# Moving the matrix combinations, a third gate and the squares of a group norm around the end of a state-space mixer

## The chip, the cores and the metric

The kernel runs on one core of a Trainium2 chip. A core has a matrix engine (TensorE, PE in the profile; PEld is its weight load), a vector engine (VectorE, DVE), an activation engine (ScalarE, ACT), GpSimd (POOL) and a sync engine (SP) that mostly issues transfers; a transfer can be issued from the SP, ACT and POOL queues. Each engine runs its own queue in the order in which the program was built, and waits on semaphores of the others. The metric is the device time of one execution in microseconds (us), as the median of several executions.

## The reference: what is computed

One layer of an encoder trunk on 512 prompt tokens and 64 sample tokens (T = 576 columns), with d_model 1024, everything in fp32. One wide projection of the normed input feeds three branches, which are merged and projected:

```python
proj = rmsnorm(x) @ w_in        # 1024 x 13344, split into
# glu_v, glu_g, conv_gate, z, xbc, dt_raw, q, xa_gate, gates
u = glu_v * sigmoid(glu_g)                       # branch A
c = causal_dwconv31(u)
c = silu(layernorm(c)) * silu(conv_gate); out_a = c @ conv_out_w
y = ssd_scan(silu(conv4(xbc)), dt, ...)          # branch B, 4 groups of 512 channels
y = (y + xh * D) * silu(z)
yg = y * rsqrt(mean(y * y, per group of 512))    # grouped RMS norm
out_b = (yg * ssd_norm_w) @ ssd_out_w
out_c = (attention(q, mem) * silu(xa_gate)) @ xa_out_w   # branch C
m = g0 * out_a + g1 * out_b + g2 * out_c
out = x + rmsnorm(m @ w_out)
```

## The kernel before

**Tiles.** Channels lie on the 128 partitions, tokens along the free dimension, so a projection onto 128 output channels is one "job": a weight tile of 1024 x 128 against the normed input `hT` (8 blocks of 128 rows by 576 tokens). Every fp32 operand is split into a high and a low part (`hi`/`lo`, `whi`/`wlo`, `hT[0]`/`hT[1]`), and `mac` (L214) issues three products for each block, on two halves of 288 tokens: 48 matmuls of 128 x 288 for a job. `W(name)` (L207) hands out a job's weights and prepares those of the job two places further in the list `order`: a load on SP into `raw`, a copy to `whi` on ACT (L193), and then `wlo`, either by a subtraction on DVE (L195) or by a copy on ACT (L197) and an accumulating transfer that POOL issues (L198). Each of these tiles has three buffers.

**Stages.** First the four groups g = 0 to 3 of the state-space mixer, each of five chunks (`chunk_a`, `chunk_b`; the last matmuls of a chunk are those of L603, into `pd`). Between the chunks stand `fills`: jobs for the gate z, the next group's B, C and x, and, for g = 3, the output projections of group 2 (`out_b(2, q)`, jobs `ob2_0` to `ob2_3`) and three gated units of branch A (`glu(j)`: jobs `gg{j}` and `gv{j}`, a tanh on ACT, a product on DVE into the tile `u`). A finished `u` puts the 31 taps of its depthwise convolution into the list `bg`; `bgrun(n)` takes the next n of them and gives them a low priority, so that they fill DVE's time (L760, here called taps). 240 taps are to be done before branch A's layer norm.

Behind the last chunk of a group stand `gating_a(g)` (y times z on DVE, L635; squares on ACT, summed on DVE into `tot`, L641; `tot` split into `th` and `tl`) and `gating_b(g)`: the sum over channels by matmuls with ones (L666, L667), a square root on ACT (L669), a reciprocal on DVE (L674), four scalings on DVE (L678) and the splits into `hi` (ACT, L620) and `lo` (DVE, L622). `out_b(3, q)`, jobs `ob3_0` to `ob3_3`, multiply these. For g = 3 the jobs `cg0` to `cg2` of the convolution's gate (`cg_spill`, with L827 on ACT and L828 on DVE) stand around `gating_b(3)`, and `cg3` behind `ob3_3`.

**Combinations.** Thirty-four jobs that follow (`gg3` to `gv7`, the gates g1 and g2, the attention's gate) are computed in pairs with seven half-sized products instead of eight (`product`, L950). This needs four sums and differences of quarters of `hT`, `T1` to `T4`: DVE adds (L852), subtracts (L861 to L869), and each result is split (`put`: ACT L857, DVE L858). The loop over `kp` does this in two halves, before `out_b(3, 0)`.

**Behind it** come the pairs, the attention over four heads, the projections `oc0` to `oc7` with `merge`, then `cg7` and `g0_0` to `g0_7`, under which the layer norm of branch A runs: the sum `csum` goes through ones matmuls (`ln_sum`, L1322 and L1323) to a mean (L1328), squares, a second `ln_sum`, a square root (L1340), a reciprocal (L1341), and eight products that are split for `oa0` to `oa7`. The last stage is `w_out` and the closing norm.

**Order.** The program text gives priorities; a list scheduler places each instruction on its engine, except where the text pins it (`keep_in_program_order`, as for the taps). So an edit of the text can also move instructions that it does not name.

Of the kernel before, what the change touches and what calls it, by code (L numbers as in the profile page):

```python
# [8 lines left out]
F32 = mybir.dt.float32  # L9
# [6 lines left out]
T = 576  # L16
# [12 lines left out]
def hybrid_trunk_kernel(  # L29
# [9 lines left out]
    nc = tc.nc  # L39
# [51 lines left out]
    spill = {k: dram.tile([8, 128, T], F32, name=f"spill_{k}") for k in ("xg", "g2", "cg")}  # L91
# [25 lines left out]
    def glu_jobs(j):  # L117
        wjob(f"gg{j}", w_in, C_GG + 128 * j)
        wjob(f"gv{j}", w_in, C_GV + 128 * j)

    for g in range(4):
        f = [("z", 4 * g + j) for j in range(4)]
        if g > 0:
            f += [("o", q) for q in range(4)]
        if g < 3:
            f += [("B", g + 1), ("C", g + 1), ("x", 4 * g + 4), ("x", 4 * g + 5)]
        f.sort(key=lambda e: "zBoCx".index(e[0]))
        if g == 3:
            z_, o_ = f[:4], f[4:]
            f = [("u", 0), z_[0], ("u", 1), z_[1], o_[0], z_[2], ("u", 2), o_[1], z_[3], o_[2], o_[3]]  # L130
        fills.append(f)
        for k, i in f:
            if k == "z":
                z_job(i)
            elif k == "o":
                ob_job(g - 1, i)
            elif k == "u":
                glu_jobs(i)
            else:
                wjob(f"{k}{i}", w_in, {"B": C_B, "C": C_C, "x": C_X}[k] + 128 * i)  # L140
        if g < 3:
            for j in (4 * g + 6, 4 * g + 7):
                wjob(f"x{j}", w_in, C_X + 128 * j)

    for j in range(3):
        wjob(f"cg{j}", w_in, C_CG + 128 * j)
    for q in range(4):
# [90 lines left out]
    def v2(ap):  # L238
# [4 lines left out]
    s2 = st.enter_context(tc.tile_pool(name="s2", bufs=2, reuse_waits="tile"))  # L243
# [11 lines left out]
        out=mask, in_=mask, pattern=[[1, 128]], compare_op=ALU.is_ge, fill=0.0,  # L255
# [75 lines left out]
    def tr_act(tiles, k, dst, wcol, ncols):  # L331
# [18 lines left out]
        out=after, in_=after, pattern=[[-1, 128]], compare_op=ALU.is_ge, fill=0.0,  # L350
# [280 lines left out]
    def gating_a(g):  # L631
        ys = [gx[4 * g + j][:, 0:T] for j in range(4)]
        tot = s2.tile([128, T], F32, tag="tot", name="tot", bufs=1)
        for j in range(4):
            nc.vector.tensor_tensor(ys[j], ys[j], gz[4 * g + j], ALU.mult)  # L635
            if j == 0:
                nc.scalar.activation(tot, ys[j], AF.Square)
            else:
                sq = s2.tile([128, T], F32, tag="gsq", name="gsq", bufs=1)
                nc.scalar.activation(sq, ys[j], AF.Square)  # L640
                nc.vector.tensor_tensor(tot, tot, sq, ALU.add)  # L641
        th = hl[0].tile([128, T], F32R, tag="hi", name="th")
        tl = hl[0].tile([128, T], F32R, tag="lo", name="tl")
        nc.scalar.activation(th, tot, AF.Copy)
        nc.vector.tensor_tensor(tl, tot, th.bitcast(F32), ALU.subtract)
        gtot[g] = (ys, th, tl)
# [61 lines left out]
    def bgrun(n):  # L708
        with tc.high_priority(offset=-150):
            for _ in range(min(n, len(bg))):  # L710
                bg.pop(0)()
# [21 lines left out]
    def glu(j, pool, tag, bufs):  # L733
        pg = proj(f"gg{j}", HB)
        t = pool.tile([128, T], F32, tag=tag, name=tag, bufs=bufs)
        nc.scalar.activation(v2(t[:, 0:512]), pg[:, :, 0:256], AF.Tanh, scale=0.5)
        nc.scalar.activation(t[:, 512:T], pg[:, 1, 256:320], AF.Tanh, scale=0.5)
        pv = proj(f"gv{j}", HB)

        def gate(a, b):  # L740
            nc.vector.scalar_tensor_tensor(v2(a), v2(t[:, 0:512]), 1.0, pv[:, :, 0:256], ALU.add, ALU.mult)
            nc.vector.scalar_tensor_tensor(b, t[:, 512:T], 1.0, pv[:, 1, 256:320], ALU.add, ALU.mult)

        u_tile(j, t, gate)
# [31 lines left out]
    def push_conv(*js):  # L776
        for ops in zip(*[conv_ops(j) for j in js]):
            bg.extend(ops)
# [10 lines left out]
    for g in range(4):  # L789
        f = [lambda k=k, i=i: fill_job(g, k, i) for k, i in fills[g]]  # L790
# [33 lines left out]
    def cg_spill(j):  # L824
        pt = proj(f"cg{j}")
        t = sx.tile([128, 640], F32, tag="bc", name="bc", bufs=4)[:, 0:T]
        nc.scalar.activation(v2(t), va(pt), AF.Tanh, scale=0.5)  # L827
        nc.vector.scalar_tensor_tensor(v2(t), v2(t), 1.0, va(pt), ALU.add, ALU.mult)  # L828
        nc.scalar.dma_start(out=spill["cg"][j], in_=t)
        bgrun(3)  # L830

    cg_spill(0)
    gating_b(3)
    cg_spill(1)
# [5 lines left out]
        return hT[0][:, ks, ts], hT[1][:, ks, ts]  # L840

    comb = {k: tuple(tcp.tile([128, 4, 288], F32R, name=f"{k}{a}", bufs=1) for a in "hl") for k in ("T1", "T2", "T3", "T4")}
    for kp in range(2):
        ks = slice(2 * kp, 2 * kp + 2)

        def blk(i, j):
            if j == 1:
                f = s2.tile([128, 582], F32, tag="xp", name="xp")[:, 0:T].rearrange("p (k t) -> p k t", k=2)
            else:
                f = s2.tile([128, T], F32, tag="acc", name="f", bufs=2).rearrange("p (k t) -> p k t", k=2)  # L850
            h, l = hb(i, j)
            nc.vector.tensor_tensor(f, h[:, ks].bitcast(F32), l[:, ks].bitcast(F32), ALU.add)  # L852
            return f

        def put(name, f):
            h, l = comb[name]
            nc.scalar.activation(h[:, ks], f, AF.Copy)  # L857
            nc.vector.tensor_tensor(l[:, ks], f, h[:, ks].bitcast(F32), ALU.subtract)  # L858

        a, b = blk(0, 1), blk(0, 0)  # L860
        nc.vector.tensor_tensor(b, b, a, ALU.subtract)  # L861
        put("T1", b)
        c = blk(1, 1)
        nc.vector.tensor_tensor(a, c, a, ALU.subtract)
        put("T3", a)
        nc.vector.scalar_tensor_tensor(c, b, -1.0, c, ALU.mult, ALU.subtract)
        put("T2", c)
        d = blk(1, 0)
        nc.vector.scalar_tensor_tensor(d, c, -1.0, d, ALU.mult, ALU.subtract)  # L869
        put("T4", d)  # L870
    for q in range(4):
        out_b(3, q)
        bgrun(2)
    st.close()
    cg_spill(3)

# [153 lines left out]
    for p in range(np_):  # L1032
        f = at[p, "P2"]
# [51 lines left out]
    for s, dst in ((0, o_csp), (1, o_css)):  # L1085
# [4 lines left out]
        for r in range(3):  # L1090
            nc.sync.dma_start(
                out=dst[0, 0, r].rearrange("(j c) -> j c", c=128), in_=tb[24 * r:24 * r + 24]
# [100 lines left out]
    def att_scores(h, khi, klo, qhi, qlo, ckh, ckl):  # L1193
        vv = token_major(None, o_mv, h, v_proj(h))
        vhl = hilo(a1, [128, 2, 256], "vv", vv)
        Ps = []
        for tp in range(3):
            ps = ps_tile()
            cnt = 2 if tp < 2 else 1
            n = 128 if tp < 2 else 64  # L1200
            for t in range(cnt):
                t0 = 256 * tp + 128 * t
                kh_, kl_ = (khi, klo) if tp < 2 else (ckh, ckl)
                mac1(
                    ps[:n, 256 * t:256 * t + 256],
                    [(qhi[:, i, t0:t0 + n], qlo[:, i, t0:t0 + n], kh_[:, i], kl_[:, i]) for i in range(2)],
                )
            Ps.append(softmax(ps, n, cnt))
            bgrun(2)
        return vhl, Ps  # L1210

    def att_pt(h, Ps):
# [89 lines left out]
    def merge(j, br, gname, oname, act, ob=ob):  # L1302
        if gname is None:
            t = sx.tile([128, 640], F32, tag="bc", name="bc", bufs=4)[:, 0:T]
            nc.sync.dma_start(out=t, in_=spill["g2"][j])
        else:
            t = gname
        pt = proj(oname, act=act)
        bgrun(5)
        nc.vector.scalar_tensor_tensor(v2(t), v2(t), 1.0, va(pt), ALU.add, ALU.mult)  # L1310
        nc.vector.tensor_tensor(ob[:, j], ob[:, j], t, ALU.add)

# [13 lines left out]
    def ln_mean():  # L1326
        for pt, (s, n) in zip(ln_sum(), HA):
            nc.scalar.activation(mean[:, s:s + n], pt[:, :n], AF.Copy, scale=1.0 / D)  # L1328
        for j in range(8):
            nc.vector.tensor_tensor(cact[j], cact[j], mean, ALU.subtract)  # L1330
            if j == 0:
                nc.scalar.activation(csum, cact[j], AF.Square)
            else:
                sq = e2.tile([128, NC], F32, tag="lsq", name="lsq")[:, 0:T]
                nc.scalar.activation(sq, cact[j], AF.Square)
                nc.vector.tensor_tensor(csum, csum, sq, ALU.add)
# [8 lines left out]
    sgs = {4 + i: t for i, t in enumerate(sgl)}  # L1345
# [5 lines left out]
        else:  # L1351
            g0t.append(gate_t(f"g0_{j}", 0, j, hlA, "lo", 8))

    for j in range(4):
        sgs[j] = hlA.tile([128, T], F32, tag="hi", name="hi", bufs=8)
        nc.sync.dma_start(out=sgs[j], in_=spill["cg"][j])
    bgrun(10000)
    late_job(*late[0])
    late_job(*late[1])
    ln_mean()  # L1360
    for e in late[2:5]:
        late_job(*e)
    ln_rstd()
# [155 lines left out]
```

## Time and profile before

| | |
|---|---|
| median of 3 runs | 1129.82 us (1129.18 to 1131.78) |
| the profiled execution, its own time | 1130.53 us |
| its span, first to last instruction | 1128.8 us |
| PE busy | 1091.0 us (97%) |
| DVE busy | 862.8 us (76%) |
| ACT busy | 607.7 us (54%) |
| POOL busy | 133.2 us (12%) |
| mean granted TensorE clock | 0.989 of full speed |

Busy time is the sum over instructions of an engine, with overlaps counted once; the rest of the span is idle. The granted clock has two levels, 1.00 (2.4 GHz) and 0.5 (1.2 GHz). A row of a timeline gives the start and the length in us, the engine, the line, the operation, output<-inputs, shapes and how many; in brackets, where there was one, the idle time ahead of it and what ended it.

### The profile page before, as it was taken

The page shows a single profiled execution, that of the slowest core. Times are in us where ns is not written, and L with a number is a line of the kernel's source. Part 1 is how long each engine was busy: PE and PEld are TensorE (multiplying, and loading weights), DVE is VectorE, ACT ScalarE, POOL GpSimd, SP SyncE. Part 2 cuts the span into 40 slices and gives each one's busy share as a digit, 9 for nine tenths or more (in the row PEclk, how much of TensorE's full clock was granted, in tenths as well). Part 3 has the DMA queues.
Part 4 walks back from the last instruction along what each step waited for, and adds up shares of the span by engine and source line. Part 5 has one row for each costly group of instructions (what it writes and reads, how often), then busy time and mean ns, then how long its engine had stood idle before and what let it go on. Part 6 is the DMA issues. An engine that isn't in the chain of part 4 may idle for free.

```text
span 1128.8 us, 20472 instructions
## 1 busy us (share of the span) xinstructions
PE 1091.0 (97%) x8081; PEld 1047.3 (93%) x8081; DVE 862.8 (76%) x1370; ACT 607.7 (54%) x1069; POOL 133.2 (12%) x230
## 2 busy tenths in 40 slices
PE   8999999999999999968998999999999999999997
PEld 8999999999999999968998999999899999999974
DVE  5778898578867878796888989849788789475533
ACT  5654675456437642362666576656445733674331
POOL 0100120012002100012121331100000111111000
PEclk9999999999999999988999999999999999999999
DMA  7354433442354633473867767757556889868912
GB/s 206 95 156 124 138 114 104 127 117 80 95 144 112 149 96 99 113 172 74 191 177 203 161 145 199 208 164 198 151 155 159 185 225 223 201 161 184 252 39 84
DMA packets 202213, 168.74 MB, mean 149 GB/s; under 512 B 15014, under 2 KB 175822, under 8 KB 202118
## 3 DMA queue, kind: packets, MB, share of 16 engines
q1 hardware_dynamic: 188294, 128.77, 39.4%
q0 software_dynamic: 12096, 35.13, 17.2%
q10 hardware_dynamic: 1728, 3.54, 0.8%
q8 instruction: 63, 1.03, 0.4%
q14 instruction: 32, 0.26, 0.1%
HBM read 117.08 MB, written 15.21 MB: 117 GB/s over the span
## 4 chain that ended last, share of the span: by engine, by line
PE 85%; DVE 6%; DMA 4%; ACT 2%; issue 1%; SPq 0%; DVEq 0%; ACTq 0%; POOLq 0%
PE mm L218 51%; PE X L950 9%; PE Y L950 5%; PE ps L218 4%; PE ps L1165 2%; PE ps L1166 2%; PE Z L950 2%; PE ps L1164 2%; PE ps L577 2%; PE ps L603 1%; PE ps L581 1%; DVE c L760 1%; DMA ob<-in_x_prompt_dram 1%; PE ps L542 1%; DMA wlo<-raw 1%
## 5 line engine op out<-in xcount | busy, mean ns | idle before, releaser
L218 PE MATMUL mm<-hT,whi 128*128 128x288 f32 (+2 forms) x2240 | 399.4, 298 | 1.7 <-ACT ob L689 0.7
L218 PEld LDWEIGHTS mm<-hT,whi 128*128 128x128 f32 x2240 | 334.2, 189 | 5.6 <-issue 2.2
L218 PE MATMUL mm<-hT,wlo 128*128 128x288 f32 (+2 forms) x1120 | 246.2, 298 | 0.0
L193 ACT ACTIVATE whi<-raw 128x1024 fp32r<-128x1024 f32 x118 | 124.7, 1057 | 196.5 <-PE mm L218 166.1
L760 DVE SCALAR_TENSOR_TENSOR c<-u,dww,c 128x606 f32<-128x606 f32 x240 | 202.1, 845 | 2.3
L218 PEld LDWEIGHTS mm<-hT,wlo 128*128 128x128 f32 x1120 | 184.7, 189 | 0.8 <-issue 0.6
L218 PE MATMUL mm<-hi,whi 128*128 128x288 f32 x512 | 112.2, 301 | 8.1 <-ACT hi L620 7.8
L195 DVE TENSOR_TENSOR wlo<-raw,whi 128x1024 fp32r<-128x1024 f32 x68 | 83.0, 1220 | 41.4 <-ACT whi L193 41.4
L218 PE MATMUL mm<-lo,whi 128*128 128x288 f32 x512 | 110.8, 298 | 1.6 <-DVE lo L622 1.6
L218 PE MATMUL mm<-hi,wlo 128*128 128x288 f32 x512 | 110.6, 297 | 0.8 <-DMA wlo<-raw 0.8
L218 PEld LDWEIGHTS mm<-hi,whi 128*128 128x128 f32 x512 | 83.1, 191 | 9.4 <-ACT hi L620 8.1
L198 POOL DMA_DIRECT2D wlo<-raw x50 | 43.9, 878 | 389.5 <-ACT wlo L197 286.7
L218 PEld LDWEIGHTS mm<-lo,whi 128*128 128x128 f32 x512 | 83.4, 190 | 1.9 <-DVE lo L622 1.9
L218 PEld LDWEIGHTS mm<-hi,wlo 128*128 128x128 f32 x512 | 83.2, 189 | 1.2 <-DMA wlo<-raw 1.0
L197 ACT ACTIVATE wlo<-raw 128x1024 fp32r<-128x1024 f32 x50 | 52.4, 1048 | 21.9 <-PE ps L218 21.9
L470 DVE SCALAR_TENSOR_TENSOR acc<-xp,scw,acc 128x579 f32<-128x579 f32 x72 | 58.3, 814 | 5.2 <-ACT acc L466 4.1
L917 ACT ACTIVATE ph<-rawb 128x512 fp32r<-128x512 f32 x34 | 21.5, 632 | 52.1 <-PE Z L950 22.4
L933 DVE TENSOR_TENSOR wlo<-sm,whi 128x1024 fp32r<-128x1024 f32 x34 | 41.5, 1220 | 4.5 <-ACT whi L932 4.4
L462 POOL COPY tails<-xp 128x3 f32<-128x3 f32 x24 | 18.3, 762 | 191.7 <-ACT xp L460 186.4
L932 ACT ACTIVATE whi<-sm 128x1024 fp32r<-128x1024 f32 x34 | 35.9, 1056 | 7.3 <-PE X L950 3.5
L691 DVE TENSOR_TENSOR ob<-ob,mm 128x576 f32<-128x576 f32 x24 | 18.0, 751 | 19.7 <-PE mm L218 19.6
L563 ACT ACTIVATE M<-R,tok 128x128 f32<-128x128 f32 (+1 forms) x80 | 24.8, 380 | 13.1 <-PE ps L603 13.1
(375 smaller groups left out, 2248.6 us busy)
## 6 DMA issues: line engine op xcount, KB each, us to landing
raw<-in_w_in_dram SPq DMA_DIRECT2D x70, 512.0 KB
wlo<-raw POOLq DMA_DIRECT2D x50, 512.0 KB, 5.6
raw<-in_w_in_dram SPq DMA_DIRECT2D x34, 256.0 KB
rawb<-in_w_in_dram SPq DMA_DIRECT2D x34, 256.0 KB
R<-scr SPq DMA_DIRECT2D x16, 512.0 KB
raw<-in_ssd_out_w_dram SPq DMA_DIRECT2D x16, 512.0 KB
raw<-in_xa_kv_w_dram SPq DMA_DIRECT2D x16, 512.0 KB
pl<-raw POOLq DMA_DIRECT2D x17, 256.0 KB, 3.7
```

The source lines that it names most:

```text
L193: a = nc.scalar.activation(hi[:, :n_], raw[:, :n_], AF.Copy)
L195: b = nc.vector.tensor_tensor(lo[:, :n_], raw[:, :n_], hi[:, :n_].bitcast(F32), ALU.subtract)
L197: nc.scalar.activation(lo[:, :n_], raw[:, :n_], AF.Copy, scale=-1.0)
L198: nc.gpsimd.dma_start(out=lo[:, :n_], in_=raw[:, :n_], accum_op=ALU.add)
L218: m = nc.tensor.matmul(o, lhsT=w, rhs=r[:, s:s + w_], start=(i == 0 and a == 0), stop=(i == n - 1 and a == 2),)
L470: nc.vector.scalar_tensor_tensor(acc, xp[:, r:r + 579], w4[:, r, jt:jt + 1], acc, ALU.mult, ALU.add)
L563: nc.scalar.activation(M[:, 4 + e, :], R[:nl, 4 + e, :], AF.Relu, scale=-1.0, bias=tok[:nl, 0, c, a + 4:a + 5])
L577: nc.tensor.matmul(pS, lhsT=bt[:nl], rhs=xw[:nl], start=True, stop=True)
L760: nc.vector.scalar_tensor_tensor(c, upad[j][:, r:r + NC], w31[:, r, j:j + 1], c, ALU.mult, ALU.add)
L932: nc.scalar.activation(hi, sm, AF.Copy)
L933: nc.vector.tensor_tensor(lo, sm, hi.bitcast(F32), ALU.subtract)
L950: nc.tensor.matmul(o, lhsT=w[:, k], rhs=r[:, k], start=(start and k == 0 and a == 0), stop=(k == 3 and a == 2), skip_group_check=True,)
```

## The change

Five edits:

- The gated unit `glu(2)` (96 matmuls) leaves the fills of g = 3 and stands behind the last chunk and `gating_a(3)`, ahead of `cg_spill(0)`; its weights move in `order` accordingly.
- The squares of the group norm for j = 2 go into a tile of their own (`gsq2`, in the buffers of `acc`), so that they alternate with `gsq`.
- The two halves of the combinations become a function `combine(kp)`, called behind `out_b(3, 0)` and `out_b(3, 1)` in the text.
- Taps: none inside `cg_spill` and `out_b(3, q)`, three behind `cg_spill(3)`; in the attention's scores 3, 3 and 2 instead of 2, 2 and 2; six instead of five in each merge.
- The four loads of `cg` tiles from DRAM stand behind `ln_mean()` instead of ahead of the rest of the taps.

```diff
-            f = [("u", 0), z_[0], ("u", 1), z_[1], o_[0], z_[2], ("u", 2), o_[1], z_[3], o_[2], o_[3]]
+            f = [("u", 0), z_[0], z_[1], ("u", 1), o_[0], z_[2], o_[1], z_[3], o_[2], o_[3]]
...
+    glu_jobs(2)
     for j in range(3):
         wjob(f"cg{j}", w_in, C_CG + 128 * j)
...
-                sq = s2.tile([128, T], F32, tag="gsq", name="gsq", bufs=1)
+                if j == 2:
+                    sq = s2.tile([128, T], F32, tag="acc", name="gsq2", bufs=2)
+                else:
+                    sq = s2.tile([128, T], F32, tag="gsq", name="gsq", bufs=1)
...
         nc.scalar.dma_start(out=spill["cg"][j], in_=t)
-        bgrun(3)
-
+
+    glu(2, s2, "acc", 2)
+    push_conv(2)
     cg_spill(0)
     gating_b(3)
...
-    for kp in range(2):
+    def combine(kp):
         ks = slice(2 * kp, 2 * kp + 2)
...
     for q in range(4):
         out_b(3, q)
-        bgrun(2)
+        if q < 2:
+            combine(q)
     st.close()
     cg_spill(3)
+    bgrun(3)
...
             Ps.append(softmax(ps, n, cnt))
-            bgrun(2)
+            bgrun(3 if tp < 2 else 2)
...
         pt = proj(oname, act=act)
-        bgrun(5)
+        bgrun(6)
...
-    for j in range(4):
-        sgs[j] = hlA.tile([128, T], F32, tag="hi", name="hi", bufs=8)
-        nc.sync.dma_start(out=sgs[j], in_=spill["cg"][j])
     bgrun(10000)
     late_job(*late[0])
     late_job(*late[1])
     ln_mean()
+    for j in range(4):
+        sgs[j] = hlA.tile([128, T], F32, tag="hi", name="hi", bufs=8)
+        nc.sync.dma_start(out=sgs[j], in_=spill["cg"][j])
```

What the scheduler makes of it, at three places (lines of the changed kernel are 1 to 8 higher).

PE, from the last matmul ahead of the norm's sums in group 3 to the first output projection, before; `hT` matmuls are those of `cg2`, `hi` and `lo` those of `ob3_0`:

```order
L218 MATMUL mm<-hT_93,whi 128x288 x2
L218 MATMUL mm<-hT_92,wlo 128x288 x2
L666 MATMUL ps<-th,onesr 128x288 x2
L667 MATMUL ps<-tl,onesr 128x288 x2
L218 MATMUL mm<-hi,whi 128x288 x4
L218 MATMUL mm<-lo,whi 128x288 x2
```

The same sums in the changed kernel, where the first three rows end `cg0` and the `hT` rows behind L670 begin `cg1`:

```order
L219 MATMUL mm<-hT_92,whi 128x288 x2
L219 MATMUL mm<-hT_93,whi 128x288 x2
L219 MATMUL mm<-hT_92,wlo 128x288 x2
L670 MATMUL ps<-th,onesr 128x288 x2
L219 MATMUL mm<-hT_92,whi 128x288 x2
L219 MATMUL mm<-hT_93,whi 128x288 x2
L219 MATMUL mm<-hT_92,wlo 128x288 x2
L219 MATMUL mm<-hT_92,whi 128x288 x2
L219 MATMUL mm<-hT_93,whi 128x288 x2
L219 MATMUL mm<-hT_92,wlo 128x288 x2
L219 MATMUL mm<-hT_92,whi 128x288
L671 MATMUL ps<-tl,onesr 128x288 x2
```

Behind the last chunk PE now has, in this order: 11 matmuls left of `gg2` and 48 of `gv2`, `cg0`, the sums of `th`, 13 of `cg1`, the sums of `tl`, the other 35 of `cg1`, `cg2`, `ob3_0`. Ahead of the last chunk's L603 it has 37 matmuls of `gg2` where it had all 96 of `gg2` and `gv2`.

DVE, up to the low parts for `ob3_0` in the kernel before; `rs` is the group norm's factor, `xs` the gated outputs, `c` a tap:

```order
L828 SCALAR_TENSOR_TENSOR bc<-bc,mm 128x576
L869 SCALAR_TENSOR_TENSOR f<-xp,f 128x576
L645 TENSOR_TENSOR tl<-tot,th 128x576
L760 SCALAR_TENSOR_TENSOR c<-u,dww,c 128x606
L858 TENSOR_TENSOR T2l<-xp,T2h 128x576
L858 TENSOR_TENSOR T4l<-f,T4h 128x576
L760 SCALAR_TENSOR_TENSOR c<-u,dww,c 128x606
L674 RECIPROCAL rs<-rs 128x576
L760 SCALAR_TENSOR_TENSOR c<-u,dww,c 128x606
L678 SCALAR_TENSOR_TENSOR xs<-xs,vecs,rs 128x576 x4
L760 SCALAR_TENSOR_TENSOR c<-u,dww,c 128x606
L622 TENSOR_TENSOR lo<-xs,hi 128x576 x4
```

DVE from the same reciprocal on in the changed kernel:

```order
L678 RECIPROCAL rs<-rs 128x576
L863 TENSOR_TENSOR T4l<-f,T4h 128x576
L857 TENSOR_TENSOR xp<-hT_92,hT_93 128x576
L866 TENSOR_TENSOR f<-f,xp 128x576
L832 SCALAR_TENSOR_TENSOR bc<-bc,mm 128x576
L682 SCALAR_TENSOR_TENSOR xs<-xs,vecs,rs 128x576 x4
L857 TENSOR_TENSOR f<-hT_92,hT_93 128x576
L869 TENSOR_TENSOR xp<-xp 128x576
L863 TENSOR_TENSOR T1l<-f,T1h 128x576
L832 SCALAR_TENSOR_TENSOR bc<-bc,mm 128x576
L623 TENSOR_TENSOR lo<-xs,hi 128x576 x2
L871 SCALAR_TENSOR_TENSOR xp<-f,xp 128x576
```

The taps have left this stretch; the second half of the combinations and the products of `cg1` and `cg2` (L832) now stand between the reciprocal and the low parts. On ACT the square root follows the copy of `whi` and `wlo` for `ob3_0`, the tanh of `cg0` and two high parts of the combinations, all of it behind `cg0`; the table for tanh is loaded anew at `cg1` instead of at `cg3`.

DVE at the last merge (`oc7`) in the kernel before, where `csum` is what the layer norm starts from:

```order
L760 SCALAR_TENSOR_TENSOR c<-u_7576,dww,c 128x606 x4
L1310 SCALAR_TENSOR_TENSOR bc<-bc,mm 128x576
L1311 TENSOR_TENSOR ob_10595<-ob_10595,bc 128x576
L772 TENSOR_TENSOR csum<-csum,u_7576 128x576
L1319 TENSOR_TENSOR sl<-csum,sh 128x576
L480 SCALAR_TENSOR_TENSOR hi<-hi,mm 128x576
```

DVE at the same merge in the changed kernel:

```order
L1318 SCALAR_TENSOR_TENSOR bc<-bc,mm 128x576
L764 SCALAR_TENSOR_TENSOR c<-u_7559,dww,c 128x606
L1319 TENSOR_TENSOR ob_10586<-ob_10586,bc 128x576
L764 SCALAR_TENSOR_TENSOR c<-u_7559,dww,c 128x606 x6
L481 SCALAR_TENSOR_TENSOR hi<-hi,mm 128x576
L764 SCALAR_TENSOR_TENSOR c<-u_7559,dww,c 128x606 x4
L776 TENSOR_TENSOR csum<-csum,u_7559 128x576
L1327 TENSOR_TENSOR sl<-csum,sh 128x576
```

Eleven taps now stand behind the last merge's first product, where there were none. On PE the first sums of the layer norm stand behind `g0_1` and 10 matmuls of `g0_2` instead of behind `g0_0`, that is 58 matmuls later, and the second sums behind 11 matmuls of `g0_5` instead of `g0_4`, 48 later; nine jobs (`cg7`, `g0_0` to `g0_7`) stand ahead of `oa0` as before.

## Rows read from the trace of the kernel before

**Rows 1.** The page, part 1: busy us of each engine, share of the span, instructions.

```profile
PE 1091.0 (97%) x8081; PEld 1047.3 (93%) x8081; DVE 862.8 (76%) x1370; ACT 607.7 (54%) x1069; POOL 133.2 (12%) x230
```

**Rows 2.** Stretches: engines' busy us (instructions), PE's granted clock, DMA share, GB/s.

```profile
498.00:511.00 13.00, 1.38 (x4) 0.80 (x4) 13.00 (x15) 6.34 (x10) 0.85 (x1) 0.59 0.63 167
511.00:518.00 7.00, 5.06 (x21) 4.71 (x22) 6.93 (x11) 2.36 (x4) 3.73 (x8) 0.53 0.00 0
518.00:548.00 30.00, 30.00 (x227) 30.00 (x227) 17.77 (x24) 9.97 (x13) 4.29 (x6) 1.00 0.65 141
745.00:907.00 162.00, 157.74 (x1198) 153.01 (x1197) 129.41 (x204) 91.81 (x180) 9.51 (x11) 0.99 0.67 172
```

**Rows 3.** Timeline of PE, end of the mixer, first pair, layer norm.

```profile
477.57 0.68 PE L603 MATMUL ps<-M,xd 64*64 64x64 f32 x16
...
497.23 0.42 PE L218 MATMUL mm<-hT,wlo 128*128 128x288 f32 x2
499.64 0.53 PE L666 MATMUL ps<-th,onesr 128*128 128x288 f32 x2 [2.00 <-ACT th L644]
502.73 0.85 PE L667 MATMUL ps<-tl,onesr 128*128 128x288 f32 x2 [2.55 <-DVE tl L645]
511.37 1.33 PE L218 MATMUL mm<-hi,whi 128*128 128x288 f32 x4 [7.78 <-ACT hi L620]
514.27 0.85 PE L218 MATMUL mm<-lo,whi 128*128 128x288 f32 x2 [1.57 <-DVE lo L622]
...
549.78 0.54 PE L950 MATMUL X<-hT,ph 128*128 128x288 f32 x2 [0.79 <-DVE bc L828]
...
971.28 0.30 PE L1322 MATMUL ps<-sh,onesr 128*128 128x288 f32 x1
...
1017.11 0.43 PE L218 MATMUL mm<-hi,whi 128*128 128x288 f32 x2
```

**Rows 4.** Timeline of DVE, the same stretches.

```profile
481.32 2.76 DVE L635 TENSOR_TENSOR xs<-xs,sz 128x576 f32<-128x576 f32 x4
...
505.45 3.75 DVE L674 RECIPROCAL rs<-rs 128x576 f32<-128x576 f32 x1
509.11 0.75 DVE L760 SCALAR_TENSOR_TENSOR c<-u,dww,c 128x606 f32<-128x606 f32 x1
509.78 3.00 DVE L678 SCALAR_TENSOR_TENSOR xs<-xs,vecs,rs 128x576 f32<-128x576 f32 x4
512.70 0.85 DVE L760 SCALAR_TENSOR_TENSOR c<-u,dww,c 128x606 f32<-128x606 f32 x1
513.46 2.76 DVE L622 TENSOR_TENSOR lo<-xs,hi 128x576 fp32r<-128x576 f32 x4
516.13 2.62 DVE L760 SCALAR_TENSOR_TENSOR c<-u,dww,c 128x606 f32<-128x606 f32 x3
...
961.17 0.76 DVE L772 TENSOR_TENSOR csum<-csum,u 128x576 f32<-128x576 f32 x1 [0.74 <-ACT u L768]
...
1025.14 0.76 DVE L624 SCALAR_TENSOR_TENSOR lo<-hi 128x576 fp32r<-128x576 f32 x1 [0.75 <-ACT hi L620]
```

**Rows 5.** Timeline of ACT, the same stretches.

```profile
497.43 1.06 ACT L193 ACTIVATE whi<-raw 128x1024 fp32r<-128x1024 f32 x1 [0.22 <-PE mm L218]
498.39 0.63 ACT L827 ACTIVATE bc<-mm 128x576 f32<-128x576 f32 x1
498.92 0.67 ACT L644 ACTIVATE th<-tot 128x576 fp32r<-128x576 f32 x1
...
502.74 1.28 ACT L669 ACT_TABLE_LOAD   x1
504.04 0.89 ACT L669 ACTIVATE rs<-ps,eps 128x288 f32<-128x288 f32 x2
...
546.99 1.28 ACT L827 ACT_TABLE_LOAD   x1
```

**Rows 6.** The chain that ended last, in order of time, at the first output projections of branch A.

```profile
1031.46 38.66 PE mm L218 x288
```

## The prediction

> **What bounds the kernel now.** I read the page's busy times first. PE is busy for 1091.0 of 1128.8 us [rows 1], and the change leaves every matmul in place, so all that can be won is PE's idle time and the time in which it runs at the lower clock. The stretches then show where that lies: in 498 to 511 PE is busy for 1.38 of 13 us, and in 511 to 518 its clock is 0.53 [rows 2]; of the 37.8 us in which PE is idle in all, 13.6 lie there. PE's timeline gives the anatomy of that hole. The last chunk's matmuls end at 477.57 + 0.68 = 478.25 (call this E), `cg0` to `cg2` follow without a gap until 497.65, and then PE waits 2.00 us for `th`, 2.55 for `tl`, 7.78 for the first `hi` and 1.57 for the first `lo`: 13.9 us [rows 3]. The first matmul on a `lo`, from which on PE runs through, is at 514.27, that is E + 36.0. DVE in the same stretch is busy without a break (13.00 of 13) [rows 2], and the rows show what it does: between the reciprocal at 505.45 and the low parts at 513.46 stand two taps [rows 4]. So the hole is a chain through a full DVE, not a lack of weights.
>
> A price that I use throughout: 227 matmuls in 30.00 us [rows 2], 0.132 us each, 6.3 us for a job of 48.
>
> **The change, part by part.**
>
> *The third gated unit as cover.* Ahead of the last chunk's L603 PE has 37 matmuls in place of 96; these 59 fewer bring E forward by 59 x 0.132 = 7.8 us. They come back behind the last chunk. Counted from the new E, `cg0` ends after 11 + 48 + 48 matmuls, at 14.1 us, and `cg2` after 96 more and the four matmuls of the sums, at 27.3.
>
> *The sums.* DVE reaches the four products with z 3.1 us behind E and ends them at 5.8 (481.32 and 2.76 long) [rows 4]. Behind them it has three taps, three additions and the product of the gated unit, about 5.2 us at 0.67 to 0.76 each, so `tot` is complete near 11, `th` (0.67 on ACT [rows 5]) near 12 and `tl` near 13.6. PE wants them at 14.1 and 16.1. The waits of 2.00 and 2.55 us go. The second tile for the squares belongs here: without it each square waits for the addition before; I give it no price of its own. If this cover failed, the loss would be bounded by these two waits.
>
> *The factor.* What is late next is ACT. Its square root is queued behind work that waits for the end of `cg0`: `whi` for `ob3_0` (0.96 from start to start), the tanh (0.53), `wlo` (0.96 as `whi`), two high parts of the combinations (0.67 each, as for `th`), the table load (1.30 from its start to that of the root) and the root (0.89) [rows 5]. That is 6.0 us, so the root is there at 14.1 + 6.0 = 20.1. Then DVE: the reciprocal, 3.66 from start to start; four other entries at 0.67 (a quarter of 513.46 to 516.13), 2.7; the scalings, 2.92; four more entries, 2.7; and 0.8 from the start of the first `lo` to PE's use of it [rows 3, 4]. The first matmul on a `lo` can start 20.1 + 3.7 + 2.7 + 2.9 + 2.7 + 0.8 = 32.9 us behind the new E. So PE still waits from 27.3 to 32.9, 5.6 us with four matmuls on `hi` inside. Behind that point both kernels do the same 44 matmuls. The gain is 7.8 + (36.0 - 32.9) = **10.9 us**.
>
> The clock fell while PE stood nearly idle from 497.65 on, and it was back at 1.00 behind 518 [rows 2, 3]. I take it that it falls again in the 5.6 us that are left, with the same slow start. If it doesn't, more is won: at 0.53 over 7 us some 6.6 us were slow, that is until about 517.6, of which 3.3 us lie behind 514.27, and half of that, 1.7 us, would be saved. The Trainium skill, "TensorE: Matmul & The Clock Gate", Part 1, calls the lower rate the default, which activity releases; by that rule the slow start comes back, as I assume, and the trace of before agrees with it.
>
> The Trainium skill, "ScalarE: Activation LUTs", *What ACT_TABLE_LOAD costs*, gives 1283 ns for a load and a drain of 1380 ns besides. Here the load takes 1.28 us and the root starts 1.30 behind its start [rows 5], so no drain shows between them. By the page's figure the factor would be 1.4 us later and the whole sum 1.4 us longer.
>
> *Combinations and taps.* The second half of the combinations costs nothing of its own: it is in the eight entries above, and its first use is in the pairs, behind 240 matmuls. If PE weren't waiting there, they would be free on a DVE without taps. Twenty taps leave the stretch of `cg_spill` and `out_b(3, q)`. Three return behind `cg3`, eight in the scores, eight in the merges. A merge then has six taps and two products, 6 x 0.76 + 2 x 0.67 = 5.9 us, under a job of 6.3: hidden. In the attention PE is idle for 4.3 of 162 us and DVE busy for 129.4 [rows 2]; eight taps are 6.1 us. Between 0 and 6.1 I take **0.8** (one tap), since DVE has 32 us free there.
>
> *The table load.* At the first pair PE waits 0.79 us for L828 of `cg3` [rows 3], which was behind a load of tanh's table at 546.99 [rows 5]. That load moves to `cg1`, where ACT has time: **-0.8**.
>
> *The layer norm.* Here the change takes back. Eleven taps (8.4 us) stand behind the last merge's first product, so `csum`, at 961.17 before [rows 4], comes near 970, and later still if ACT's two copies stand behind a weight copy. But PE's place for the first sums is also 58 matmuls, 7.7 us, later than 971.28 [rows 3], at 979.0, so it is that place which decides, and the second sums stand 48 matmuls, 6.3 us, later. All that follows hangs on them: the last `lo`, done at 1025.14 + 0.76 = 1025.9 [rows 4], comes at 1032.2. PE, though, is at `oa0` at 1017.11 [rows 3] with the same nine jobs ahead. The last 8 matmuls of `oa0` and `oa1` need that `lo`; they end near 1033.4 and `oa2` starts near 1033.8 instead of 1031.46 [rows 6]. I take **+2.4**; the ends are 0 and 7.7.
>
> The loads of `cg` behind `ln_mean` free SP's queue for weights at the merges; the products that need them are more than 40 us later, so they cost nothing unless they land behind the mean's chain.
>
> *Sum.* -10.9 + 2.4 + 0.8 - 0.8 = -8.5 us. The profiled execution took 1130.53 us (1128.8 of span and 1.7 around it), so 1122.0. That execution was 0.7 above the median of the three runs; I leave 1122.0.
>
> **Rivals.** No change is to be told from one below 0.2%, 2.3 us.
>
> 1. *Better than summed.* The clock holds and the scheduler's places in the layer norm hide the taps: 1130.5 - 10.9 - 1.7 - 0.8 = 1117.1. For it: the 5.6 us wait is broken up by matmuls on `hi`. Against it: DVE has no break between reciprocal and `lo` in the sum.
> 2. *The taps show.* All eight in the attention are on the path: 5.3 more, 1127.3. For it: in 745 to 907 PE already waits, 4.3 us. Against it: DVE's idle 32 us.
> 3. *The wait only moves.* The root slips behind `cg1` instead of `cg0`, since ACT waits in order; then all is 6.3 later, 1128.3, no difference that can be told. Against it: the sums of `tl` end near 16.4, 1.5 us ahead of ACT's table load.
> 4. *Slower.* The layer norm's chain slips: its copies of the last convolution output stand on ACT behind weight copies that wait for PE, and PE's sums wait in order with the rest of the gate jobs behind them. Each job of slip adds 6.3 us that nothing hides. From 10.8 us on, two jobs, the kernel is slower: 1122.0 + 12.6 = 1134.6. Against it: `csum` has 9 us until PE's place.
> 5. *A drain behind the table load*: 1123.4. By [rows 5] it does not show.
>
> **How the numbers follow.** My forecast has 0.55 with 1119 to 1125.5; the first rival 0.12, the second 0.13, the third 0.12, the slower one 0.06, the drain 0.02. The first, the second and the drain lie with the forecast on the faster side, 0.82; the third is "same", 0.12; the fourth slower, 0.06. A range of 1116.5 to 1128 leaves out the fourth, most of the third and a little below the first.
>
> **What would show it.** In the changed kernel's trace: no wait of PE at the two sums (L670, L671); the end of `cg2` near 498 and one wait of 5 to 6 us ahead of `ob3_0`, released by `hi` and `lo`; PE's clock at 0.5 shortly behind it; the pairs 11 us earlier; waits of some 2 to 3 us in all at `oa0` and `oa1`, released by DVE or ACT; PE's idle time in the attention near 5 us. I am wrong if the wait ahead of `ob3_0` is above 9 us or below 3, or if the layer norm costs more than 5.

## The result, and the profile after

The changed kernel takes 1134.41 us (median of 17 runs, 1130.53 to 1139.26), the kernel before 1128.69 beside it (17 runs, 1126.82 to 1132.74). The ratio is 1.0051, 95% interval 1.0037 to 1.0064: slower by half a per cent, where 8.5 us of gain were forecast. The profiled execution took 1131.46 us, the second lowest of the 17, so some 3 us of the loss don't show in its trace.

The page's busy times and the four stretches of [rows 1] and [rows 2], now of the changed kernel:

```profile
PE 1094.0 (97%) x8081; PEld 1049.6 (93%) x8081; DVE 863.5 (76%) x1370; ACT 606.9 (54%) x1069; POOL 137.2 (12%) x230
```

```profile
498.00:511.00 13.00, 9.74 (x72) 9.26 (x70) 12.32 (x15) 10.53 (x15) 1.72 (x2) 0.99 0.87 208
511.00:518.00 7.00, 6.39 (x27) 6.22 (x28) 6.66 (x10) 3.02 (x5) 5.72 (x6) 0.52 0.98 231
518.00:548.00 30.00, 30.00 (x227) 29.82 (x225) 11.84 (x17) 10.41 (x14) 3.76 (x7) 1.00 0.69 152
745.00:907.00 162.00, 158.22 (x1204) 153.71 (x1203) 137.63 (x215) 92.69 (x181) 9.53 (x11) 0.99 0.66 172
```

From 498 to 511 PE is busy for 9.74 us where it was for 1.38: most of the hole has been filled. PE's timeline at the same places as [rows 3], and ahead of them:

```profile
163.33 0.76 PE L219 MATMUL mm<-hT,whi 128*128 128x288 f32 x4 [1.39 <-DVE sz L481]
...
276.23 0.78 PE L219 MATMUL mm<-hT,whi 128*128 128x288 f32 x4 [2.46 <-DVE sz L481]
...
386.61 0.33 PE L543 MATMUL ps<-ident,xs 128*128 128x128 f32 x1 [0.78 <-DVE xs L474]
387.71 0.79 PE L219 MATMUL mm<-hT,whi 128*128 128x288 f32 x4 [0.77 <-ACT acc L741]
...
465.03 0.66 PE L524 MATMUL ps<-ident,hin 128*128 128x128 f32 x4 [2.50 <-DMA hin<-in_state_ssm_dram]
...
478.75 0.68 PE L604 MATMUL ps<-M,xd 64*64 64x64 f32 x16
...
506.77 0.43 PE L219 MATMUL mm<-hT,wlo 128*128 128x288 f32 x2
510.41 0.54 PE L219 MATMUL mm<-hi,whi 128*128 128x288 f32 x2 [3.20 <-ACT hi L621]
511.61 0.85 PE L219 MATMUL mm<-hi,whi 128*128 128x288 f32 x2 [0.66 <-DVE bc L832]
512.28 0.85 PE L219 MATMUL mm<-lo,whi 128*128 128x288 f32 x2
...
1020.76 0.53 PE L219 MATMUL mm<-hi,wlo 128*128 128x288 f32 x2 [2.49 <-DMA wlo<-raw]
```

E, the end of the last chunk, is at 478.75 + 0.68 = 479.43. Before it was at 478.25 [rows 3], and 470.5 was forecast. Behind E all goes as worked out: the first `lo` matmul at 512.28 is 32.85 us behind E, forecast 32.9. So of this execution's miss of 9.5 us (1131.46 against 1122.0) 9.0 lie ahead of E, most of it in waits that the kernel before did not have: PE waits for a product of z (`sz`) in groups 1 and 2, for two inputs in chunk 0 of group 3, and for the state that chunk 4 of group 3 loads.

Counted from one group's last L604 (L603 before) to the next one's, groups 1, 2 and 3 took 104.5, 110.3 and 131.2 us before and 105.9, 112.5 and 129.5 after. Group 3, with 59 matmuls fewer, should be 7.8 shorter and is only 1.6 shorter.

### The profile page after: what moved, and what is told of

The parts are those of the page before. It is cut to its first block, busy times and chain, and to the rows that moved or that the text cites. A ratio compares the mean times of both kernels' runs of the same rounds, so it can differ in the third digit from the quotient of the medians.

```text
span 1129.8 us, 20482 instructions
## 1 busy us (share of the span) xinstructions
PE 1094.0 (97%) x8081; PEld 1049.6 (93%) x8081; DVE 863.5 (76%) x1370; ACT 606.9 (54%) x1069; POOL 137.2 (12%) x230
## 4 chain that ended last, share of the span: by engine, by line
PE 85%; DMA 5%; DVE 5%; ACT 2%; issue 2%; SPq 0%; DVEq 0%; POOL 0%; ACTq 0%; POOLq 0%
PE mm L219 52%; PE X L958 9%; PE Y L958 4%; PE ps L219 4%; PE ps L1173 2%; PE ps L1174 2%; PE ps L1172 2%; PE Z L958 2%; PE ps L578 1%; PE ps L604 1%; DMA wlo<-raw 1%; PE ps L582 1%; DMA out_dram<-ho 1%; DMA ob<-in_x_prompt_dram 1%; DVE xs L682 1%
## 5 line engine op out<-in xcount | busy, mean ns | idle before, releaser
L463 POOL COPY tails<-xp 128x3 f32<-128x3 f32 x24 | 14.6, 608 | 189.1 <-ACT xp L461 183.2
```

## The experiments

Two theories stood at the start. **A**: the second tile for the squares, which the diff puts into all four groups, makes the scheduler write groups 0 to 3 in another order, and that order's waits eat the gain. **B**: the gated unit that left the fills of group 3 was cover there, and its waits come from that.

### Undoing and isolating the two

**e1_squares_alone** is the kernel before with this one edit:

```diff
-                sq = s2.tile([128, T], F32, tag="gsq", name="gsq", bufs=1)
+                if j == 2:
+                    sq = s2.tile([128, T], F32, tag="acc", name="gsq2", bufs=2)
+                else:
+                    sq = s2.tile([128, T], F32, tag="gsq", name="gsq", bufs=1)
```

> The kernel before with one edit of the change, the squares of one product in `acc`'s two buffers, in all four groups. Theory A (the second tile for the squares makes the scheduler write groups 0 to 3 in another order, whose waits eat what the hole gives): E, the end of the last chunk's L603, comes 2.5 to 5 us later than in the kernel before, with PE waits near 148, 162 and 274 us as in the changed kernel, and the time is 2 to 5 us longer, 1131 to 1134. Rival B (the gated unit that left the fills of group 3 is what costs): within 1 us of the kernel before, E at 478 to 479.5.

Measured: 1138.45 us, ratio 1.0087 (1.0062 to 1.0112), E 11.5 us later than before in the profiled execution, which at 1143.81 us is the slowest of six. A's direction, at about twice its upper bounds. PE's longest waits and one more: engine and line, what they were waited for, us in all, times, the longest.

```profile
PE mm L218 <- ACT hi L620: 12.0, 1, 12.0
PE mm L218 <- DVE sz L480: 4.2, 2, 2.8
PE mm L218 <- DVE lo L622: 3.6, 1, 3.6
...
PE mm L218 <- ACT acc L740: 1.7, 1, 1.7
```

The first and the third stand in the hole behind E; the two waits for `sz`, in groups 1 and 2, and the one for `acc`, in group 3, stand ahead of it.

**e2_squares_last_group** is the changed kernel with that condition narrowed:

```diff
-                if j == 2:
+                if j == 2 and g == 3:
```

> The changed kernel with the second tile for the squares in group 3 alone; groups 0 to 2 are then in the order of the kernel before. Theory A: E 6 to 9 us earlier than in the changed kernel (470.5 to 473.5) and the time 6 to 9 us shorter, 1125 to 1128. Rival B: only the 2.8 us of drift that the changed kernel collects by the start of group 3 come back, E near 476.6, the time 2 to 4 us shorter than the changed kernel's, and the waits of chunk 0 and chunk 4 of group 3 stay.

Measured: 1127.80 us, 0.9988 (0.9971 to 1.0005), 6.6 below the changed kernel. E is at 471.3, as A has it, and the two waits in chunk 0 of group 3 are gone, but the wait for the state stays, at 2.30 us, as B has it. Both are at work.

**e3_unit_alone** is the kernel before with the gated unit alone moved, its weights too:

```diff
-            f = [("u", 0), z_[0], ("u", 1), z_[1], o_[0], z_[2], ("u", 2), o_[1], z_[3], o_[2], o_[3]]
+            f = [("u", 0), z_[0], z_[1], ("u", 1), o_[0], z_[2], o_[1], z_[3], o_[2], o_[3]]
...
+    glu_jobs(2)
...
+    glu(2, s2, "acc", 2)
+    push_conv(2)
     cg_spill(0)
```

> The kernel before with the third gated unit alone moved behind the last chunk; squares, combinations, taps and the loads of `cg` as before. Theory A: E near 470.5 to 472, PE's hole ahead of ob3_0 shorter, the time 3 to 8 us shorter than before's. Rival B: waits in chunks 0 and 4 of group 3 (an input from DVE or ACT, and the load of the chunk's state) of 3 us or more, E later than 473, and a time within 3 us of before's.

Measured: 1130.59 us, 1.0010 (0.9996 to 1.0025): no gain, as B says, and E at 475.25. Chunk 0 has none of the waits that B names; the one long new wait ahead of E is this:

```profile
460.87 0.75 PE L524 MATMUL ps<-ident,hin 128*128 128x128 f32 x4 [4.74 <-DMA hin<-in_state_ssm_dram]
```

**e4_state_own_buffer** is the changed kernel with

```diff
-            hin = sc.tile([128, 4, 128], F32, tag="hio", name="hin", bufs=1)
+            hin = sc.tile([128, 4, 128], F32, tag="hin3" if g == 3 else "hio", name="hin", bufs=1)
```

> The changed kernel with a buffer of its own for the state that chunk 4 of group 3 loads (`hin`), so that the load needn't wait until the store of `ho` has left the shared one; up to chunk 3 of group 3 the order is that of the changed kernel. If the 2.50 us wait at 462.52 and the half clock behind it (1.7 us) are a cost of their own: both are gone, E is 3 to 4.5 us earlier (475 to 476.5), and the time is 3 to 4.5 us shorter than the changed kernel's. If something else is late at the same place (the state's own chain): the wait turns up under another name and the time is within 1 us.

Measured: 1128.99 us, 0.9997 (0.9985 to 1.0009), 5.4 below the changed kernel; the wait is gone and E at 476.1, as expected; the time gains 0.9 us more than that. SP's queue shows what the load had waited for, in the changed kernel:

```profile
456.77 0.37 SPq L184 DMA_DIRECT2D raw<-in_w_in_dram  x1
457.23 0.53 SPq L503 DMA_DIRECT2D out_dram<-ho  x1
461.71 0.37 SPq L519 DMA_DIRECT2D hin<-in_state_ssm_dram  x1
```

The load of `hin` can go only when the store of `ho`, which uses the same buffer, has read it: 4.5 us behind the store's issue, which stands right behind a weight load. In the kernel before there was no slack here either. The same queue and PE's timeline of the kernel before:

```profile
458.49 0.38 SPq L502 DMA_DIRECT2D out_dram<-ho  x1
460.85 0.37 SPq L518 DMA_DIRECT2D hin<-in_state_ssm_dram  x1
```

```profile
463.67 0.43 PE L218 MATMUL mm<-hi,wlo 128*128 128x288 f32 x2
463.94 0.60 PE L523 MATMUL ps<-ident,hin 128*128 128x128 f32 x4
```

PE arrives 3.1 us behind the issue; in the changed kernel the transposes start 3.3 us behind it (465.03 against 461.71), after a wait. By the trace's DMA packets the load ends at 463.40 before and at 464.64 in the changed kernel, 0.5 us ahead of the transposes where PE did not wait and 0.4 where it did. So the state came just in time before, and any step that brings chunk 4 forward runs into it.

### Both causes away, and each edit by itself

**e5_both_mended** has the edits of e2 and of e4.

> The changed kernel with the second tile for the squares in group 3 alone, and the state's own buffer in group 3. Theory (two causes ahead of E, nothing else: the squares' tile in groups 0 to 2, and the load of the state that chunk 4 of group 3 waits for): E at 468.5 to 470, no PE wait over 1 us between 300 and 495 us, and 1122.5 to 1125.5 us, 9 to 12 below the changed kernel. Rival (the hole takes back what comes early, as it did not shrink by more than the wait's place): E as early, but the wait ahead of ob3_0 grows by the same amount, and the time is 1127 or more.

Measured: 1118.64 us, 0.9921 (0.9909 to 0.9934). E is at 468.42; ahead of it no wait of over 0.6 us is left behind 15 us. The rest of the hole, in PE's timeline:

```profile
467.74 0.68 PE L604 MATMUL ps<-M,xd 64*64 64x64 f32 x16
...
500.41 0.53 PE L219 MATMUL mm<-lo,whi 128*128 128x288 f32 x2 [3.57 <-DVE lo L623]
...
507.94 0.53 PE L219 MATMUL mm<-hi,whi 128*128 128x288 f32 x2 [0.99 <-DVE ob L695]
...
533.62 0.42 PE L958 MATMUL Z<-hT,ph 128*128 128x288 f32 x2
```

The theory of two causes holds, and the time is 4 us below its bounds. The two profiled executions are 13.5 us apart (1131.46 and 1117.99): 11.0 lie ahead of E, 1.6 between E and the first pair (the last row, 65.2 us behind E; 66.8 in the changed kernel), 0.9 behind it. The other 2.3 us of the medians show in no trace. The clock is hardly a part of it. It was 1.00 from 495 to 520 here and 0.93 in e11 (below), whose edit stands behind this stretch and which still takes only 65.3 us from E to the first pair; e5 has a wait of 0.99 us there that e11 does not have, and by these numbers it took back what the clock gave.

**e7_unit_and_state** has the edits of e3 and of e4, on the kernel before.

> The kernel before with the third gated unit moved, as in e3_unit_alone, and the state's own buffer in group 3. If e3's 4.74 us wait for the state and the half clock behind it are all that kept the move from paying: E at 468.5 to 470.5, and 1123.5 to 1126 us, 5 to 7 below e3. Its hole keeps e3's waits (1.02, 6.41 and 2.91 us), since combinations and taps are where they were; against e5 it shows what those edits give in the hole, by the sum some 4 to 6 us. If the move itself is worth nothing: 1128 or more.

Measured: 1122.86 us, 0.9946 (0.9933 to 0.9958). The unit's move is worth 5 to 6 us once the state's load is out of the way; without that, nothing. The own buffer without the move was not run; in the kernel before no PE wait for the state shows that it could remove.

**e12_unit_state_squares** adds the squares' second tile in group 3 to e7.

> The kernel of e7_unit_and_state with the second tile for the squares in group 3; combinations, taps and the loads of `cg` as in the kernel before. It splits the 4.2 us between e7 and e5. If taps and combinations gave them: the wait ahead of ob3_0 stays at 7 us or more, and 1121.5 to 1123. If the squares did: that wait falls to 4 to 5 us, and 1118 to 1120.

Measured: 1118.06 us, 0.9902 (0.9888 to 0.9916). The squares give what was open between e7 and e5. ACT's timeline shows how, first e7 (its profiled execution, 1126.54 us, is the slowest of five), then e12:

```profile
486.47 0.67 ACT L645 ACTIVATE th<-tot 128x576 fp32r<-128x576 f32 x1
...
493.82 1.28 ACT L670 ACT_TABLE_LOAD   x1
495.12 0.89 ACT L670 ACTIVATE rs<-ps,eps 128x288 f32<-128x288 f32 x2
```

```profile
478.74 0.67 ACT L648 ACTIVATE th<-tot 128x576 fp32r<-128x576 f32 x1
...
486.36 1.28 ACT L673 ACT_TABLE_LOAD   x1
487.66 0.50 ACT L673 ACTIVATE rs<-ps,eps 128x288 f32<-128x288 f32 x1
```

With one buffer each square waits for the addition before, `th` starts 17.1 us behind E (469.40) and the root 25.7; with two, 10.1 and 19.1 (E at 468.60). The root has slipped by a whole job without the second tile: that is the prediction's third rival, and the second tile is what keeps it away. The other edits that e5 has beyond e12 (combinations, taps, loads of `cg`) bring nothing in sum: 1118.64 us against 1118.06, ratios 0.9921 against 0.9902. By the traces they win and lose. The first pair in e12:

```profile
536.86 0.42 PE L956 MATMUL Z<-hT,ph 128*128 128x288 f32 x2
```

That is 68.3 us behind E, 3.1 more than in e5; yet both spans are 1116.3 us. So e5 loses behind the pairs what it wins ahead of them, 2.04 us of it in a wait at `oa0` that e12 does not have (see the layer norm).

### Why the second tile costs in groups 0 to 2

**e8_squares_own_buffer** is e1 with a second tile that shares no buffer with the convolutions:

```diff
-                    sq = s2.tile([128, T], F32, tag="acc", name="gsq2", bufs=2)
+                    sq = s2.tile([128, T], F32, tag="gsq2", name="gsq2", bufs=1)
```

> The kernel before with the squares of one product in a second buffer of their own, in all four groups, in place of `acc`'s. If it was the sharing of `acc`'s two buffers with the convolutions that cost e1_squares_alone its 9.6 us: within 2 us of the kernel before, and E within 1.5 us. If it is the order that the scheduler writes once squares and sums need no longer alternate: as e1, 1134 to 1140, with PE waits for the silu product (L481 in the changed kernel's lines) in groups 1 and 2.

Measured: 1136.07 us, 1.0068 (1.0051 to 1.0086), E 5.5 us later than before in the profiled execution, the slowest of six. PE waits 2.01 us for the product of z in group 2, and 0.83 in group 1, which the trace puts down to `ssm`, the instruction right behind that product on DVE. So the sharing is not it; what is left is the order. DVE's timeline in the changed kernel, ahead of the wait that ends at 163.33, and then in the kernel before at the same place:

```profile
158.31 1.22 DVE L196 TENSOR_TENSOR wlo<-raw,whi 128x1024 fp32r<-128x1024 f32 x1
159.45 0.15 DVE L675 TENSOR_TENSOR ssm<-ssm 128x2 f32<-128x2 f32 x1
159.52 3.00 DVE L682 SCALAR_TENSOR_TENSOR xs<-xs,vecs,rs 128x576 f32<-128x576 f32 x4
162.43 0.75 DVE L481 SCALAR_TENSOR_TENSOR sz<-sz,mm 128x576 f32<-128x576 f32 x1
```

```profile
158.07 1.22 DVE L195 TENSOR_TENSOR wlo<-raw,whi 128x1024 fp32r<-128x1024 f32 x1
159.20 0.74 DVE L480 SCALAR_TENSOR_TENSOR sz<-sz,mm 128x576 f32<-128x576 f32 x1
159.87 3.00 DVE L678 SCALAR_TENSOR_TENSOR xs<-xs,vecs,rs 128x576 f32<-128x576 f32 x4
```

The product of z reads the tile `mm`, in PSUM, the memory that matmuls write to, and PE wants that tile for its next job. Before, it stood ahead of the four scalings of the group norm; now it stands behind them, 3.2 us later, and PE waits 1.39 us for the tile.

**e9_squares_groups_0_3** and **e10_squares_groups_2_3** are e5 with another condition, the first line added in e9, the second in e10:

```diff
-                if j == 2 and g == 3:
+                if j == 2 and g in (0, 3):
+                if j == 2 and g > 1:
```

> The kernel of e5_both_mended with the second tile for the squares in group 0 too. In e4 (all groups) group 1 is 1.9 us longer than in e5, group 2 3.7 and group 3 2.1, counted between the last L604 of each. If each group's squares cost the group behind them on their own: here group 1 is 1.5 to 2.5 us longer than in e5, with the 1.39 us wait for the silu product near 161, groups 2 and 3 are as in e5 within 0.5, and the time is 1120 to 1122. If only the late groups' tiles cost: no wait near 161, and 1117.5 to 1119.5.

> The kernel of e5_both_mended with the second tile for the squares in group 2 too. If each group's squares cost the group behind them: groups 1 and 2 as in e5 within 0.5 us, two waits of 0.8 us in chunk 0 of group 3 near 384, group 3 1.5 to 2.5 us longer, and 1120 to 1122. If the 2.48 us wait near 273 in group 2 is group 2's own doing: that wait is here as well, and the time is 1122 or more.

Measured: e9 1121.33 us, 0.9934 (0.9917 to 0.9951); group 1 takes 106.1 us against e5's 104.2, with the 1.39 us wait (162.75), and groups 2 and 3 are e5's within 0.4. e10 1124.70 us, 0.9959 (0.9945 to 0.9973); group 3 takes 124.9 against 122.9, with two waits of 0.77 us in its chunk 0, and no wait near 273. So the squares of group 0 and of group 2 each delay the group behind them, and the 2.46 us wait at 276.23 is left for group 1's; this is by exclusion, as group 1's squares weren't run by themselves. e10's time is 2.7 us above the upper bound expected; its profiled execution, 1121.51, is one of its lowest and shows only 1.8 us ahead of E. What its other runs lose beyond that stays open.

### The layer norm

**e6_taps_in_scores** is e5 with the first edit, **e11_taps_at_first_queries** e5 with the second:

```diff
-            bgrun(3 if tp < 2 else 2)
+            bgrun(4)
```

```diff
             tr_act(mt_, j, memT, V_MEM, NMEM)
+            bgrun(2)
```

> The kernel of e5_both_mended with four taps behind each of the three softmaxes of a head (3, 3 and 2 there), so that no tap is left behind the last merge; PE's matmuls of the two sums of the layer norm then stand where they stood in the kernel before. If the place of the sums is what the layer norm costs (2.75 us between g0_7 and oa2 in the changed kernel): the 2.5 us wait at `oa0` is gone and the time is 2 to 3 us below e5's. If the 16 taps come onto the path of the attention: the wait is gone, but PE's idle time between 735 and 900 us grows by 2 us or more and the time is that of e5 within 1 us.

> The kernel of e5_both_mended with two taps behind each of the eight transposes of the memory ahead of the attention, where DVE is busy for 36.6 of 50 us (730 to 780); PE's sums of the layer norm stand where they stood in the kernel before. If DVE's free time takes them: the wait of 2.04 us at `oa0` is gone, no new wait ahead of 800 us, and the time is 2 to 3 us below e5's, 1115.5 to 1117. If not: PE's idle time between 720 and 900 us grows by 2 us or more, and the time is e5's within 1 us or above.

Measured: e6 1119.15 us, 0.9926 (0.9912 to 0.9939), no gain over e5; e11 1116.49 us, 0.9889 (0.9874 to 0.9904), 2.1 us below e5, the lowest median of all and 1.1% below the kernel before. The stretches 780 to 900 and 950 to 1010 of e5, e6 and e11, in this order:

```profile
780.00:900.00 120.00, 116.21 (x878) 112.18 (x878) 107.58 (x169) 69.68 (x134) 8.86 (x11) 1.00 0.65 165
950.00:1010.00 60.00, 57.69 (x421) 57.06 (x420) 40.93 (x57) 43.02 (x57) 8.14 (x9) 0.98 0.78 179
```

```profile
780.00:900.00 120.00, 114.19 (x834) 109.08 (x835) 111.28 (x172) 68.22 (x131) 8.67 (x10) 0.97 0.62 159
950.00:1010.00 60.00, 60.00 (x453) 60.00 (x452) 38.57 (x54) 44.19 (x59) 8.71 (x10) 1.00 0.78 183
```

```profile
780.00:900.00 120.00, 115.81 (x869) 110.89 (x868) 112.13 (x176) 67.80 (x130) 8.66 (x10) 1.00 0.65 164
950.00:1010.00 60.00, 59.87 (x449) 59.64 (x449) 40.59 (x57) 44.01 (x57) 8.25 (x9) 1.00 0.77 176
```

In both, PE's idle time at `oa0` and `oa1` goes (57.69 to 60.00 and 59.87 of 60): the late place of the sums is what the layer norm costs. e6 pays for it in the attention, with 2.0 us more idle time than e5 and a clock of 0.97. In e11 some of the taps run ahead of 780, where DVE is busy for 41.58 of 50 us from 730 on (36.55 in e5); its attention has 0.4 us more idle time, at full clock.

## Why the prediction was wrong

**E 7.8 us earlier: the step that failed.** The prediction's "these 59 fewer bring E forward by 59 x 0.132 = 7.8 us" takes PE's work ahead of E to be gapless and to stay so. The trace of before showed it gapless, but not how little slack stood behind that. Of the 9.0 us that are missing, 1.3 lie in group 1 and 2.2 in group 2. In group 3 it is 6.2: 0.78 + 0.77 + 2.50 of waits, and some 1.7 of clock (0.89 from 460 to 475, 11% of 15), behind the wait for the state. A start 0.7 us earlier makes up for a little. By the runs' ratios the squares in groups 0 to 2 cost some 9 us (e4 against e5), and the state's load 7 (e3 against e7) or, on the changed kernel, 6 (e4 against the changed kernel). With both away (e5) the kernel is 9.5 us below the kernel before beside it, where 8.5 were forecast; that the two are so near is in part luck, as e5's E lies 2.1 us ahead of the forecast 470.5.

**The second tile, "no price of its own".** It had two, of opposite sign: about 5 us won in group 3 (e12 against e7), about 9 lost through the groups ahead. The gain needs the unit's move: in e1, without it, the first `lo` comes 36.8 us behind E, where it came 36.0 behind in the kernel before. The tile was looked at in the one group that the prediction spoke of, though the edit stands in a function that runs four times.

**The hole.** Right in its terms. The sums no longer wait, the root ends 20.1 us behind E (499.57), as forecast, `cg2` ends at 507.20, 27.8 us behind E (forecast 27.3), the waits ahead of `ob3_0` are 3.20 + 0.66 us (forecast 5.6 in all), and the first `lo` comes where it was put. The clock fell again, to 0.52 from 511 to 518. That isn't a must: in e5, behind a wait of 3.57 us, it didn't fall. But the 1.7 us that rival 1 puts on it did not follow: e5 takes 65.2 us from E to the first pair, e11, where the clock fell, 65.3.

**The pairs 11 us earlier.** 1.0 us, since E was late; with both causes away they are 13.6 us earlier (e5, 533.62 against 547.25).

**Attention.** 0.8 us were put down as lost; PE's idle time fell from 4.3 to 3.8 of 162 us. Here DVE's free time took the taps. e6 shows how near the limit that was: four behind each softmax is too many.

**The table load.** The wait of 0.79 us at the first pair is gone, as forecast. No drain shows behind the load: the root starts 1.29 us behind it (498.68 against 497.39), the load itself 1.28. So the 1380 ns that the Trainium skill, "ScalarE: Activation LUTs", *What ACT_TABLE_LOAD costs*, adds do not show here, and rival 5 falls:

```profile
497.39 1.28 ACT L673 ACT_TABLE_LOAD   x1
498.68 0.89 ACT L673 ACTIVATE rs<-ps,eps 128x288 f32<-128x288 f32 x2
```

**Layer norm, +2.4.** Measured: 1.85 us ahead of before at the end of `g0_7`, 0.89 behind at `oa2`, so +2.7, and one wait of 2.49. Size and cause were right (e11), the last link was not: the wait ends with `wlo` of a weight, not with a `lo` of the norm. ACT copies that weight at 1017.32, behind tanhs of the norm that wait for DVE.

**The rivals.** The kernel is slower, but not by rival 4: no slip of two jobs in the layer norm. Rivals 2 and 5 did not occur; e7, without the second tile, shows rival 3's slip. All of them, and the limits that would show the prediction wrong, looked at the stretch behind E. None of these limits was crossed, and the time was still 12 us off. Two of the signs did show it, `cg2`'s end (507.20, not near 498) and the pairs. The case that was missing is that the work ahead of the hole gets slower.

## What to carry to other kernels

A gain that comes from "this point is reached earlier" is only as large as the slack of everything that has to be ready by then: read for each load and each shared buffer ahead of that point how long before its use it lands. Here the state's load was issued 3.1 us ahead of its use, in the kernel before, with nothing to spare. And an edit to a helper counts at every call: compare the order of the whole program, not just of the stretch the edit is for, since a freed buffer lets a list scheduler move unlike work ahead of what PE is waiting for.

## What was not expected of the hardware

The same wait, in the same order of instructions, cost clock in one execution and not in another. The stretch 270 to 290 of the changed kernel, with its wait of 2.46 us, and of e4, with 2.48:

```profile
270.00:290.00 20.00, 17.54 (x130) 16.68 (x129) 14.31 (x21) 7.96 (x11) 1.27 (x4) 1.00 0.26 80
```

```profile
270.00:290.00 20.00, 17.52 (x120) 17.07 (x118) 13.93 (x21) 6.99 (x10) 1.27 (x4) 0.91 0.26 80
```

The granted clock is 1.00 in the first and 0.91 in the second, where 120 matmuls are on record in place of 130. The wait of 3.57 us ahead of `ob3_0` stands in six traces: from 495 to 520 the clock was 0.93 in e4, e6, e9 and e11, 0.86 in e10, and 1.00 in e5. The Trainium skill, "TensorE: Matmul & The Clock Gate", Part 1, calls the lower rate the default, which activity releases. These rows agree in that the lower clock stands behind a wait, but a wait of the same length didn't always bring it.

Nor do such waits alone set how far runs lie apart. The 12 runs of e4, which has both these waits (2.48 and 3.57 us), lie within 2.9 us, the 12 of e10, which has lost the first, within 7.3, the 17 of the changed kernel within 8.7. The clock has a part in it: in the changed kernel's two fastest runs its mean was 0.992 and 0.993, in the two slowest 0.988. By an estimate from these, 0.0045 of 1130 us, that is some 5 of the 8.7 us. Where the clock fell in runs without a trace, and what makes up the rest, is open.
